# A two-layer attention trunk on one core: fixed tile places, memory keys in other banks, attention units in a new order, and one compressed-value product in place of four

## The chip, the cores and the metric

The kernel runs on one core of one Trainium2 chip. The metric is the device time of one execution in microseconds (us), as the median of several runs. A core has a matrix engine (PE, with its weight loads PEld), a vector engine (DVE), a scalar engine (ACT), a general engine (POOL) and a sync engine (SP), which here only issues DMAs. Each engine works through its own instructions in the order in which they were written down for it, and waits on semaphores for the others.

## What is computed

Two layers are applied to x (256 tokens, 1024 wide). In each, with h = RMSNorm(x) and z = h @ w_in:

```
o_a = nsa(q, kv, gate)       # 8 heads of 64, 2 key groups; three parts with a gate each:
                             #   compressed keys and values (15 blocks), selected blocks, a window
o_b = fox(q, k, v, f)        # 8 heads of 64, causal, with a forget bias
o_m = cross(q, mem_kv)       # 4 heads of 128 into 256 memory tokens
u   = sum over a, b, m of sigmoid(gate) * ((o * silu(.)) @ w_branch)
x   = x + u @ w_out
```

For the compressed part of `nsa` the kernel computes, for each of two groups of 128 tokens (t = 0, 1),

```
s   = einsum('bqgrd,bngd->bgrqn', qb, k_c) * scale       # n: 15 compressed blocks
p_c = masked_softmax(s, cmp_end <= t)
o_c = einsum('bgrqn,bngd->bqgrd', p_c, v_c)              # the product of the compressed values
```

where k_c and v_c come from k and v by a small two-layer network (`compress`). mem_kv = RMSNorm(mem) @ w_mem_kv gives the memory keys K and values V.

## The kernel before, in words

**Matrix products.** The large products run in `gemm_steps` (L264). An fp32 operand is split into a high and a low fp32r part, and three matmuls per 128 rows (high x high, low x high, high x low) accumulate in a bank of PSUM; `gemm` (L285) takes two banks, one for each t, from the pool `mm` (3 banks) unless another pool is given. PSUM has the pools mm (3 banks), S (2), T (2) and O (1) (L73). Weights come in granules of 256 rows and up to 512 columns: `load_w` (L123) has SP issue the DMA into one of four `wraw` tiles (L143), `split_w` (L147) has ACT write the high part `whi` (L172; L167 where a gain is multiplied in) and DVE the low part `wlo` (L173, L168). A granule is 12 matmuls.

**Order of the stages.** In a layer `mem_kv` (L466) comes first: K (L489), then V (L490). Then come the stages that `ORDER` (L30) names: K2 K1 Q (keys, values and queries of nsa), SA SB SM (silu gates, L848, 256-column matmuls), FK FQ FV (fox), MG (the first merge gate), MQ (memory queries); then branch a, b, m and w_out. A key bank of the memory is released when DVE has multiplied it with its norm (`kn`, L476), which waits for the norm `rmk` of POOL (L362 to L365).

**Units.** Attention is cut into units: scores on PE into an S bank, softmax on DVE and ACT, a last multiply of P by the inverse sum on POOL (L559), four transposes on PE (L228), a split into `PTh`/`PTl` (L382, L384), and products on PE into the O bank (L504). A queue of units is worked off in order, one is started per granule (`unit_step`, L241), and the head of the queue waits for the marks in its `deps`, with all units behind it. The queue before is: 4 units of t = 0, the compressed unit `Cmp` of t = 0, 8 units of t = 1, the `Cmp` of t = 1, the fox units, the memory units.

**The compressed unit** (L949) has 8 score matmuls (L962), a softmax, one transpose of `ce`, one 128x128 copy to `eT` (L349 on ACT or L351 on DVE, by turns) and four fp32 matmuls of 128 columns with the values `Vc` (L1003), one for each r, into one O bank. `Vc` is written in `value` (L922). The compress network runs during FK, through `compress_step` (L932) and a chain of small steps (L867 to L928).

**Tables.** While FK and the next stage run in layer 0, `smallp`, the small parameters of layer 1, is loaded (L607 to L609) once DVE has read the old ones for the last time (L908), and POOL builds 18 tables from it (L640 to L642).

**What sets the final order.** The program is written in Python in the order above; a scheduler then merges the instructions of all helpers into one order for each engine, by its own simulated times. So a change of the written order moves instructions on all engines. The pools give each tag its place in SBUF when it is first asked for.

Of the kernel before, what the change touches and what calls it, by code (L numbers as in the profile page):

```python
# [17 lines left out]
NT = 2  # L18
# [8 lines left out]
KEEP = 10  # L27
WARM = 8

ORDER = "K2 K1 Q SA SB FK MG FQ FV SM MQ".split()  # L30


def shape_constants():
    half = 32
    inv = (10000.0 ** (-np.arange(half, dtype=np.float32) / np.float32(half))).astype(np.float32)
    ang = np.arange(T, dtype=np.float32)[:, None] * inv[None, :]
    cos, sin = np.cos(ang).astype(np.float32), np.sin(ang).astype(np.float32)
    cos2 = np.concatenate([cos, cos], 1).reshape(NT, 128, 64).transpose(1, 0, 2)
    sin2 = np.concatenate([-sin, sin], 1).reshape(NT, 128, 64).transpose(1, 0, 2)
    ident = np.eye(128, dtype=np.float32)  # L40
    p = np.arange(128)
    ntri = -(p[:, None] <= p[None, :]).astype(np.float32)
    even = (p[:, None] == 2 * np.arange(64)[None, :]).astype(np.float32)
    odd = (p[:, None] == 2 * np.arange(64)[None, :] + 1).astype(np.float32)
    t = np.arange(T).reshape(NT, 128).T
    n = np.arange(15)
    cmask = np.where(16 * n[None, None, :] + 31 <= t[:, :, None], 0.0, NEG).astype(np.float32)

    bmask = 0.5 * (p[:, None] // 16 == np.arange(8)[None, :]).astype(np.float32)
    cm = np.where(p[None, :] <= p[:, None], 0.0, NEG).astype(np.float32)  # L50
# [10 lines left out]
def hybrid_kernel(ctx: ExitStack, tc, I, cst_d, out_d):  # L61
# [5 lines left out]
    def S(shape, tag, bufs=1, dt=F32):  # L67
        return sb.tile(shape, dt, tag=tag, name=tag, bufs=bufs)
# [3 lines left out]

    pmm, pS, pT, pO = bank("mm", 3), bank("S", 2), bank("T", 2), bank("O", 1)  # L73

    def T2():
        return S([128, 520], "t2", bufs=4)

    def SQ():
        return S([128, 512], "sq")
# [211 lines left out]
                between(g)  # L291


    cst = S([128, cst_d.shape[1]], "cst")
    mrow0 = S([128, NT, D], "big")

    def mem_cols(mrow, g):
# [23 lines left out]
    def take(n):  # L321
        off[0] += n
        return cst[:, off[0] - n:off[0]]
# [7 lines left out]
    bmask = take(8)  # L331
    cm = take(128)
    mhalf = S([128, 16], "mhalf")
    nc.gpsimd.memset(mhalf, -0.5)
# [131 lines left out]
    def mem_kv(l, mT, rm):  # L466
        KT = [S([128, 4, T], f"mK{i}", dt=F32R) for i in range(2)]
        V = [S([128, NT, 512], f"mV{i}", dt=F32R) for i in range(2)]

        def on_k(t, p):  # L470
            ss = ss_heads(p, 4, 128, scale=rm[t])
            r = rstd_of(ss, 128, "rmk", rm[t])

            def s1():
                kn = T2()[:, :512]
                nc.vector.tensor_tensor(heads(kn, 4), heads(p, 4), b3(r, 4, 128), op=ALU.mult)  # L476

                def s2():
                    ts = slice(t * 128, (t + 1) * 128)
                    put_T([lambda h=h: kn[:, h * 128:(h + 1) * 128] for h in range(4)],  # L480
                          lambda q: split_evac(KT[0][:, :, ts], KT[1][:, :, ts], q.rearrange("p (h t) -> p h t", h=4)))
                later(1 + t, s2)
            later(1, s1)

        def on_v(t, p):
            nc.scalar.activation(V[0][:, t], p, AF.Copy, scale=rm[t])
            nc.vector.scalar_tensor_tensor(V[1][:, t], p, rm[t], V[0][:, t].bitcast(F32), op0=ALU.mult, op1=ALU.subtract)

        gemm(mT, 8, on_k)  # L489
        gemm(mT, 8, on_v)  # L490
        return KT, V

# [100 lines left out]
    for l in range(2):  # L593
# [268 lines left out]
            mark((nm, l))  # L862


        Vc = S([128, 512], "Vc").rearrange("p (r g d) -> p r g d", r=4, g=2)

        def compress_out(i, hp):  # L867
            ch = S([128, 128], "cmph")
# [2 lines left out]
            def s1():  # L871
# [10 lines left out]
                def s2():  # L882
                    if i == 0:
                        sT = S([128, 30], "sT")
                        nc.vector.scalar_tensor_tensor(sT, th, 1.0, hs, op0=ALU.add, op1=ALU.mult)
                        later(1, lambda: key(sT))
                    else:
                        sT = S([128, 4, 2, 16], "sTv")
                        nc.gpsimd.memset(sT, 0.0)
                        nc.vector.scalar_tensor_tensor(hs, th, 1.0, hs, op0=ALU.add, op1=ALU.mult)  # L890
                        nc.vector.tensor_copy(sT[:, :, :, 0:15], heads(hs, 2)[:, None].to_broadcast([128, 4, 2, 15]))
                        later(1, lambda: value(sT))
                later(1, s2)

# [54 lines left out]
        class Cmp:  # L949
# [40 lines left out]

            def transpose(self):
                def out(q):
                    self.eT = S([128, 128], "eT")
                    evac(self.eT, q[:, 0:128])
                put_T([lambda: self.e.rearrange("p h n -> p (h n)")], out)

            def product(self):
                box = []

                def one(r):  # L1000
                    if not box:
                        box.append(pO())
                    nc.tensor.matmul(box[0][:, r * 128:(r + 1) * 128], Vc[:, r].rearrange("p g d -> p (g d)"), self.eT,  # L1003
                                     start=True, stop=True)
                for r in range(4):
                    put(lambda r=r: one(r), *([lambda: self.done(box[0])] if r == 3 else []))

        oa_ = act_pair(4, "oT")

        def nsa_units(t):  # L1010
# [7 lines left out]
                split_evac(oa_[0][:, :, ts], oa_[1][:, :, ts], s3)  # L1018
                mark(("oTa", l, t))

            deps = [("q", l, t)] + [("k", l, i, t_) for i in (1, 2) for t_ in range(t + 1)]
            res = []
            for g in range(2):
                gs = slice(g * 64, (g + 1) * 64)
                out = Out(2 if t == 0 else 4, lambda O, gs=gs: fold(sw, O, gs))
                for br in ((None,) if t == 0 else (0, 1)):
                    for r0 in (0, 2):
# [25 lines left out]
                        res.append(Unit(deps, score, *args, (0, 2, 1, 3), product))  # L1053
            res.append(Cmp(t, done_c))
            return res

# [161 lines left out]
        runs = dict(K1=run_k1, K2=run_k2, Q=run_q, MQ=run_mq,  # L1218
                    FK=lambda: gemm(hT, 8, on_fqk(fkT, False), between=compress_step),
                    FQ=lambda: gemm(hT, 8, on_fqk(fqT, True)),  # L1220
                    FV=lambda: (gemm(hT, 8, on_fv), mark(("fv", l))))
        for nm in ORDER:
# [55 lines left out]
```

## Time and profile before

| what | value |
|---|---|
| median of 3 runs | 636.09 us (635.55 to 636.16) |
| profiled execution, its own time | 636.09 us |
| its span in the trace | 634.4 us |
| PE busy | 621.8 us (98%) |
| DVE busy | 471.9 us (74%) |
| ACT busy | 382.0 us (60%) |
| POOL busy | 175.5 us (28%) |

PE is the engine of this kernel; the other engines prepare its operands. "Busy" of PE counts overlapping matmul records once, so the costs of PE work are read from the spacing of starts (a piece of the chain "start, length, what xN"), not from the mean of a record. Layer 0 takes the span up to about 306 us, and layer 1 repeats it. Engine letters, lines and shapes are as in the code; PEclk or the PEclk column is the granted clock of PE.

### The profile page before, as it was taken

What the parts mean: (1) busy time and instruction counts of PE and PEld (TensorE: products, weight loads), DVE (VectorE), ACT (ScalarE), POOL (GpSimd) and SP (SyncE); (2) the same over time, 40 slices, a digit from 0 to 9 for tenths busy, and PEclk for the clock granted to TensorE, in tenths of its full rate; (3) what the DMA queues carried; (4) which work ended last, traced back from release to release, by engine and by line L of the source; (5) the groups of instructions that cost most, each with busy time, mean ns of one, the idle gap of its engine ahead of it and who ended that gap; (6) DMA issues with size and microseconds to landing.
All of it is one profiled execution on the core that took longest, in us unless ns stands there. A gap on an engine that the chain in (4) does not pass through costs nothing.

```text
span 634.4 us, 10249 instructions
## 1 busy us (share of the span) xinstructions
PE 621.8 (98%) x3551; PEld 532.0 (84%) x3551; DVE 471.9 (74%) x844; ACT 382.0 (60%) x813; POOL 175.5 (28%) x234
## 2 busy tenths in 40 slices
PE   7899999999999999999999999999999999999997
PEld 5689998788998788888888989977889888888885
DVE  3668898668977886955577799966799678787563
ACT  5767567555666666555467656845566667664441
POOL 2813403242512320702112142141053051042130
PEclk8989999999999999999999999999999999999999
DMA  8788866275444545446855695445644465445541
GB/s 298 175 276 265 259 143 187 75 214 164 130 121 134 145 139 160 134 139 225 285 182 157 173 338 162 143 132 137 185 114 133 99 184 150 144 122 167 168 156 75
DMA packets 75189, 107.66 MB, mean 170 GB/s; under 512 B 16865, under 2 KB 30465, under 8 KB 74881
## 3 DMA queue, kind: packets, MB, share of 16 engines
q1 hardware_dynamic: 75072, 106.99, 56.7%
q8 instruction: 28, 0.46, 0.3%
q14 instruction: 25, 0.20, 0.1%
q10 hardware_dynamic: 64, 0.02, 0.0%
HBM read 103.82 MB, written 3.15 MB: 169 GB/s over the span
## 4 chain that ended last, share of the span: by engine, by line
PE 94%; DMA 3%; POOL 1%; SPq 0%; DVE 0%; issue 0%; ACT 0%; POOLq 0%
PE mm L274 60%; PE mm L848 11%; PE S L274 6%; PE T L228 6%; PE O L504 4%; PE S L1035 2%; DMA cst<-in_cst_dram 1%; PE S L1134 1%; PE S L942 1%; DMA big<-in_mem_dram 1%; PE S L1194 1%; DMA gcol<-in_fox_k_norm_dram 1%; PE S L1132 1%; PE O L1003 1%; PE S L962 1%; PE T L744 0%
## 5 line engine op out<-in xcount | busy, mean ns | idle before, releaser
L173 DVE TENSOR_TENSOR wlo<-wraw,whi 128x1024 fp32r<-128x1024 f32 (+2 forms) x160 | 200.8, 1258 | 79.9 <-ACT whi L172 78.6
L172 ACT ACTIVATE whi<-wraw 128x1024 fp32r<-128x1024 f32 (+2 forms) x160 | 166.8, 1042 | 101.7 <-PE mm L274 65.1
L274 PE MATMUL mm<-whi,aTh 128*128 128x512 f32 (+1 forms) x480 | 190.3, 399 | 2.1 <-DVE t L476 2.1
L274 PE MATMUL mm<-whi,aTl 128*128 128x512 f32 (+1 forms) x480 | 189.0, 394 | 0.3 <-DVE aTl L384 0.3
L274 PE MATMUL mm<-wlo,aTh 128*128 128x512 f32 (+1 forms) x480 | 184.6, 395 | 0.0
L559 POOL TENSOR_TENSOR P<-P,d 128x512 f32<-128x512 f32 (+1 forms) x64 | 61.1, 970 | 208.0 <-DVE d L555 104.6
L274 PEld LDWEIGHTS mm<-whi,aTh 128*128 128x128 f32 x480 | 90.5, 190 | 19.5 <-issue 3.2
L274 PEld LDWEIGHTS mm<-whi,aTl 128*128 128x128 f32 x480 | 90.8, 189 | 17.2 <-DVE aTl L384 0.7
L274 PEld LDWEIGHTS mm<-wlo,aTh 128*128 128x128 f32 x480 | 90.6, 189 | 16.8 <-issue 0.4
L848 PE MATMUL mm<-aTh,wlo 128*128 128x256 f32 x192 | 54.8, 287 | 0.0
L848 PE MATMUL mm<-aTl,whi 128*128 128x256 f32 x192 | 54.8, 286 | 0.0
L848 PE MATMUL mm<-aTh,whi 128*128 128x256 f32 x192 | 54.6, 285 | 0.0
L548 ACT ACTIVATE P<-S,m 128x256 f32<-128x256 f32 (+1 forms) x112 | 46.8, 428 | 7.4 <-DVE m L545 6.5
L1108 POOL TENSOR_TENSOR big<-big,t 128x512 f32<-128x512 f32 x16 | 27.9, 1752 | 59.2 <-DVE t L1107 54.2
L382 ACT ACTIVATE PTh<-T 128x512 fp32r<-128x512 f32 (+1 forms) x48 | 26.9, 561 | 25.6 <-PE T L228 25.4
L274 PE MATMUL mm<-whi,oTh 128*128 128x512 f32 x96 | 38.5, 404 | 0.7 <-ACT PTh L382 0.7
L274 PE MATMUL mm<-wlo,oTh 128*128 128x512 f32 x96 | 38.8, 407 | 0.0
L274 PE MATMUL mm<-whi,oTl 128*128 128x512 f32 x96 | 38.6, 402 | 0.0
L848 PEld LDWEIGHTS mm<-aTh,wlo 128*128 128x128 f32 x192 | 36.5, 191 | 0.4
L848 PEld LDWEIGHTS mm<-aTh,whi 128*128 128x128 f32 x192 | 36.6, 190 | 0.3
L848 PEld LDWEIGHTS mm<-aTl,whi 128*128 128x128 f32 x192 | 36.6, 190 | 0.2
L545 DVE TENSOR_REDUCE m<-S 128x2 f32<-128x512 f32 (+3 forms) x64 | 32.3, 515 | 2.7 <-PE S L1194 2.5
(232 smaller groups left out, 1033.0 us busy)
## 6 DMA issues: line engine op xcount, KB each, us to landing
wraw<-in_w_in_dram SPq DMA_DIRECT2D x112, 512.0 KB, 3.8
wraw<-in_w_out_dram SPq DMA_DIRECT2D x16, 512.0 KB, 4.3
wraw<-in_w_mem_kv_dram SPq DMA_DIRECT2D x15, 512.0 KB, 5.2
wraw<-in_w_branch_a_dram SPq DMA_DIRECT2D x16, 256.0 KB, 3.9
wraw<-in_w_branch_b_dram SPq DMA_DIRECT2D x8, 512.0 KB, 3.6
wraw<-in_w_branch_m_dram SPq DMA_DIRECT2D x8, 512.0 KB, 3.6
wraw<-in_w_in_dram SPq DMA_DIRECT2D x8, 408.0 KB, 4.2
wraw<-in_w_in_dram SPq DMA_DIRECT2D x8, 384.0 KB, 3.8
```

The costliest lines, as they stand in the source:

```text
L172: nc.scalar.activation(wh[:, j, :n], v[:, j, :n], AF.Copy)
L173: nc.vector.tensor_tensor(wl[:, j, :n], v[:, j, :n], wh[:, j, :n].bitcast(F32), op=ALU.subtract)
L228: nc.tensor.transpose(q[0][0:b.shape[1], i * 128:(i + 1) * 128], b, ident)
L274: mi = nc.tensor.matmul(o_, a[:, kg, ts], w_[:, k, :n], start=(kg == 0 and i == 0), stop=(last and k == 1 and i == 2))
L382: nc.scalar.activation(hi, src, AF.Copy, scale=scale)
L504: nc.tensor.matmul(self.O[0:lhsT.shape[1], cols], lhsT, rhs, start=first, stop=False, skip_group_check=True)
L545: nc.vector.tensor_reduce(m[:, n:n + c], heads(sp[:, o_:o_ + w * c], c), axis=AXX, op=ALU.max, negate=True)
L548: nc.scalar.activation(self.P[:, k], sp[:, k], AF.Exp, bias=m[:, n:n + 1], accum_out=d[:, n:n + 1])
L559: nc.gpsimd.tensor_tensor(P3, P3, b3(d[:, n:n + c], c, w), op=ALU.mult)
L848: mi = nc.tensor.matmul(o_, w_, a[:, kg, :], start=(kg == 0 and j % 2 == 0 and i == 0), stop=(kg == 7 and i == 2), skip_group_check=True)
L1035: put(lambda j=j, k_=k_: nc.tensor.matmul(sp()[:, j * 256:(j + 1) * 256], QA[:, g, r0 + j, ts], k_, start=(j == 0 and k_ is kh), stop=(j = ...
L1108: nc.gpsimd.tensor_tensor(uv, uv, tn, op=ALU.add)
```

## The change

The change has five parts.

1. Thirty tags get their places first, in one list with fixed sizes; `t2` has 512 columns and not 520, the constants' tile is 832 wide, and the mask `bmask` has 2 columns and not 8.
2. In layer 0 the memory keys accumulate in the two S banks (`bank=None if l else pS`), and V takes the mm banks.
3. The queue of units begins with the 4 units of t = 0, then the 8 of t = 1, and only then the two `Cmp` units. The 8 units wait for the end of FK by a new mark.
4. `ORDER` has MG after FQ and FV.
5. The compressed values' product is one fp32r matmul of 96 rows and 512 columns. Rows 0 to 31 hold the high part of the values against the high part of P, rows 32 to 63 high against low, rows 64 to 95 low against high. Twelve pieces of 32x128 (8 on ACT, 4 on DVE) write `eT`, now in a `PTh` tile, where one copy did.

```
-ORDER = "K2 K1 Q SA SB FK MG FQ FV SM MQ".split()
+ORDER = "K2 K1 Q SA SB FK FQ FV MG SM MQ".split()
...
-    bmask = 0.5 * (p[:, None] // 16 == np.arange(8)[None, :]).astype(np.float32)
+    bmask = 0.5 * ((p[:, None] // 16) % 2 == np.arange(2)[None, :]).astype(np.float32)
...
+    for tag, width, bufs, dt in (("cst", 832, 1, F32), ("big", 2048, 1, F32), ("wraw", 1024, 4, F32), ("whi", 1024, 3, F32R),
...
+        S([128, width], tag, bufs, dt)
...
-        gemm(mT, 8, on_k)
+        gemm(mT, 8, on_k, bank=None if l else pS)
         gemm(mT, 8, on_v)
...
-        Vc = S([128, 512], "Vc").rearrange("p (r g d) -> p r g d", r=4, g=2)
+        V3 = S([128, 128], "V3", dt=F32R)[0:96]
...
-                nc.tensor.matmul(vp[:, 0:64], sT.rearrange("p r g n -> p (r g n)"), w2[:, 1, :], start=True, stop=True)
-                nc.vector.tensor_tensor(Vc.rearrange("p r g d -> p (r g) d"), vp[:, 0:64][:, None, :].to_broadcast([128, 8, 64]), b3(bmask, 8, 64),
-                                        op=ALU.mult)
+                nc.tensor.matmul(vp[0:96, 0:64], sT.rearrange("p r g n -> p (r g n)"), w2[:, 1, :], start=True, stop=True)
+                vf = S([128, 128], "cmph")[0:96]
+                nc.vector.tensor_tensor(heads(vf, 2), vp[0:96, 0:64][:, None, :].to_broadcast([96, 2, 64]), b3(bmask[0:96], 2, 64),
+                                        op=ALU.mult)
+                nc.scalar.activation(V3, vf, AF.Copy)
+                nc.vector.tensor_tensor(V3[64:96], vf[64:96], V3[64:96].bitcast(F32), op=ALU.subtract)
...
-                    self.eT = S([128, 128], "eT")
-                    evac(self.eT, q[:, 0:128])
+                    self.eT = eT = S([128, 512], "PTh", bufs=2, dt=F32R)[0:96]
+                    for r in range(4):
+                        rs, src = slice(r * 128, (r + 1) * 128), q[r * 32:(r + 1) * 32, 0:128]
+                        nc.scalar.activation(eT[0:32, rs], src, AF.Copy)
+                        nc.vector.tensor_tensor(eT[32:64, rs], src, eT[0:32, rs].bitcast(F32), op=ALU.subtract)
+                        nc.scalar.activation(eT[64:96, rs], src, AF.Copy)
...
-                    nc.tensor.matmul(box[0][:, r * 128:(r + 1) * 128], Vc[:, r].rearrange("p g d -> p (g d)"), self.eT,
-                                     start=True, stop=True)
-                for r in range(4):
-                    put(lambda r=r: one(r), *([lambda: self.done(box[0])] if r == 3 else []))
+                    nc.tensor.matmul(O, V3, self.eT, start=True, stop=True)
+                    self.done(O)
+                put(one)
...
-        for t in range(NT):
-            units.extend(nsa_units(t))
+        nu_ = [nsa_units(t) for t in range(NT)]
+        for u_ in nu_[1][:-1]:
+            u_.deps.append(("FK", l))
+        units.extend(nu_[0][:-1] + nu_[1][:-1] + [nu_[0][-1], nu_[1][-1]])
...
+                    FK=lambda: (gemm(hT, 8, on_fqk(fkT, False), between=compress_step), mark(("FK", l))),
```

Lines from the list of tags on are 11 higher in the changed kernel (L274 becomes L285), those behind `value` some 15.

On POOL in layer 0, before: behind the norm `cr` of the compressed keys the tables of layer 1 stand in one run, and the multiplies of P of the units of t = 1 come behind them (names: Ct and St are the tables, P a unit's probabilities, rf a norm of FQ).

```order
L903 TENSOR_TENSOR cr<-cr,mhalf 30x1
L640 TENSOR_TENSOR Ct<-cst,smallp 128x64
L641 TENSOR_TENSOR St<-cst,smallp 128x32
...
L642 TENSOR_TENSOR St<-cst,smallp 128x32
L889 MEMSET sTv 128x128
L559 TENSOR_TENSOR P<-P,d 128x512 x2
```

The same place with the change: one multiply, 6 tables, one multiply, 12 tables, the four steps of FQ's norms, and the third multiply.

```order
L570 TENSOR_TENSOR P<-P,d 128x512
L651 TENSOR_TENSOR Ct<-cst,smallp 128x64
...
L653 TENSOR_TENSOR St<-cst,smallp 128x32
L570 TENSOR_TENSOR P<-P,d 128x512
L651 TENSOR_TENSOR Ct<-cst,smallp 128x64
...
L653 TENSOR_TENSOR St<-cst,smallp 128x32
L373 TENSOR_SCALAR rf<-ss 128x8
L374 TENSOR_TENSOR rf<-rf,mhalf 128x8
L373 TENSOR_SCALAR rf<-ss 128x8
L374 TENSOR_TENSOR rf<-rf,mhalf 128x8
L570 TENSOR_TENSOR P<-P,d 128x512
```

So the second and third units of t = 1 now have tables ahead of their multiply.

On PE at the start of layer 0, before, with the numbers of the tiles: mm_145 and mm_146 hold K for t = 0 and 1, mm_315 and mm_316 V. mm_316 takes the bank that mm_145 held, so that its first matmul waits for K of t = 0 to be read (L476).

```order
L274 MATMUL mm_315<-whi_319,aTh_107 128x512
L274 MATMUL mm_315<-whi_319,aTl_108 128x512
L274 MATMUL mm_316<-whi_226,aTh_107 128x512
L274 MATMUL mm_316<-whi_226,aTl_108 128x512
L274 MATMUL mm_316<-wlo_227,aTh_107 128x512
L274 MATMUL mm_316<-whi_226,aTh_107 128x512
L274 MATMUL mm_316<-whi_226,aTl_108 128x512
L274 MATMUL mm_316<-wlo_227,aTh_107 128x512
L228 MATMUL T_372<-cst_63,t2_311 128x128 x4
```

The same place with the change: both halves of V go on together, granule by granule, and the transposes of the normed keys (T_402) come 30 V matmuls behind the last of K's.

```order
L285 MATMUL mm_346<-whi_349,aTh_137 128x512
L285 MATMUL mm_346<-whi_349,aTl_138 128x512
L285 MATMUL mm_345<-wlo_350,aTh_137 128x512
L285 MATMUL mm_345<-whi_349,aTh_137 128x512
L285 MATMUL mm_345<-whi_349,aTl_138 128x512
L285 MATMUL mm_346<-wlo_350,aTh_137 128x512
L285 MATMUL mm_346<-whi_349,aTh_137 128x512
L285 MATMUL mm_346<-whi_349,aTl_138 128x512
L239 MATMUL T_402<-cst_93,t2_341 128x128 x4
```

The V matmuls of three granules now stand ahead of those transposes, in banks that K does not use.

On ACT in layer 0, with the change, the pieces of the first `Cmp` unit (L1012 and L1014, PTh 32x128) stand among other work; before there was one copy here.

```order
L1012 ACTIVATE PTh<-T 32x128
L994 ACTIVATE ce<-csm 128x8x15
L1014 ACTIVATE PTh<-T 32x128
L1012 ACTIVATE PTh<-T 32x128
L183 ACTIVATE whi<-wraw 128x1024
L559 ACTIVATE P,d<-S,m 128x128
L1014 ACTIVATE PTh<-T 32x128
L1012 ACTIVATE PTh<-T 32x128
L587 ACTIVATE tm<-O 64x512
L1108 ACTIVATE t_1930<-mm 128x512
L559 ACTIVATE P,d<-S,m 128x256
L1014 ACTIVATE PTh<-T 32x128
```

Behind these rows follow one more L1012, one L183, one L1108 and the last L1014 of the unit. On PE the unit's transpose stands 57 matmuls ahead of its product: 17 of L285 with 512 columns, 31 of L859 with 256 columns, 4 of L515, 4 of L1148 and L1150, and the transpose of the second `Cmp`.

## Rows read from the trace of the kernel before

**Rows 1.** The page: busy time by engine, and the chain's shares by engine.

```profile
PE 621.8 (98%) x3551; PEld 532.0 (84%) x3551; DVE 471.9 (74%) x844; ACT 382.0 (60%) x813; POOL 175.5 (28%) x234
...
PE 94%; DMA 3%; POOL 1%; SPq 0%; DVE 0%; issue 0%; ACT 0%; POOLq 0%
```

**Rows 2.** What PE waited for: us in total, times, longest us.

```profile
PE mm L274 <- DVE t L476: 2.1, 1, 2.1
...
PE mm L274 <- ACT PTh L382: 0.7, 2, 0.3
```

**Rows 3.** The chain in order of time: start us, length us, what.

```profile
59.22 10.92 PE mm L274 x48
...
92.86 4.91 PE mm L848 x41
...
159.16 0.89 PE O L1003 x8
```

**Rows 4.** Line L1003 on PE: duration ns min/median/max, first and last start us.

```profile
L1003 PE MATMUL O<-eT,Vc x32: 271/275/275, 159.0 to 500.1; 128*128 128x128 f32 x32
```

**Rows 5.** Timeline of the start: start us, length us, instruction [idle before <-releaser].

```profile
30.15 0.69 DVE L476 TENSOR_TENSOR t<-mm,rmk 128x512 f32<-128x512 f32 x1 [2.88 <-POOL rmk L365]
...
30.99 0.47 PE L274 MATMUL mm<-whi,aTh 128*128 128x512 f32 x1 [2.06 <-DVE t L476]
...
33.46 1.33 ACT L167 ACTIVATE whi<-wraw,gk 128x512 fp32r<-128x512 f32 x2 [1.06 <-DMA wraw<-in_w_mem_kv_dram]
...
34.01 0.63 PE L274 MATMUL mm<-whi,aTl 128*128 128x512 f32 x1
...
34.22 1.42 DVE L168 SCALAR_TENSOR_TENSOR wlo<-wraw,gk,whi 128x512 fp32r<-128x512 f32 x2 [0.70 <-ACT whi L167]
...
37.25 0.90 ACT L172 ACTIVATE whi<-wraw 128x832 fp32r<-128x832 f32 x1 [1.98 <-DMA wraw<-in_w_in_dram]
...
38.19 1.03 DVE L173 TENSOR_TENSOR wlo<-wraw,whi 128x832 fp32r<-128x832 f32 x1 [1.96 <-ACT whi L172]
...
41.51 0.35 PE L274 MATMUL mm<-wlo,aTh 128*128 128x416 f32 x1
```

**Rows 6.** Work by stretch: PE, PEld, DVE, ACT, POOL busy, PEclk, DMA share, GB/s.

```profile
31.00:70.00 39.00, 39.00 (x193) 35.09 (x194) 30.95 (x80) 24.35 (x59) 8.32 (x13) 0.96 0.88 279
```

**Rows 7.** Small reads of PSUM, lines L685 and L687: columns as in rows 4.

```profile
L685 ACT ACTIVATE KH<-T x16: 254/273/276, 57.9 to 389.6; 64x128 fp32r<-64x128 f32 x16
...
L687 DVE TENSOR_TENSOR KL<-T,KH x16: 269/285/295, 59.2 to 392.1; 64x128 fp32r<-64x128 f32 x16
```

**Rows 8.** ACT groups by form: busy us, mean ns, idle before.

```profile
L172 ACT ACTIVATE whi<-wraw 128x1024 fp32r<-128x1024 f32 x144 | 152.8, 1061 | 95.7 <-PE mm L274 62.3 <-issue 10.8 <-PE mm L848 7.5
L548 ACT ACTIVATE P<-S,m 128x256 f32<-128x256 f32 x64 | 29.7, 471 | 7.2 <-DVE m L545 6.5 <-DVE d L555 0.7
L548 ACT ACTIVATION_READ_ACCUMULATOR P<-S,m 128x1 f32 x112 | 23.0, 205 | 0.0
...
L1092 ACT ACTIVATE t<-mm 128x512 f32<-128x512 f32 x24 | 14.2, 592 | 9.3 <-PE mm L274 9.1
```

**Rows 9.** Timeline of layer 0 around the tables, of PE, SP, POOL and DVE.

```profile
124.97 0.30 PE L897 MATMUL T<-w,sT 128*30 128x64 f32 x2
...
128.24 0.34 SPq L607 DMA_DIRECT2D smallp<-in_nsa_q_norm_dram  x1
...
131.65 0.32 POOL L640 TENSOR_TENSOR Ct<-cst,smallp 128x64 f32<-128x64 f32 x1 [3.94 <-DMA smallp<-in_nsa_q_norm_dram]
131.93 0.25 POOL L641 TENSOR_TENSOR St<-cst,smallp 128x32 f32<-128x32 f32 x1
...
134.90 1.40 DVE L173 TENSOR_TENSOR wlo<-wraw,whi 128x1024 fp32r<-128x1024 f32 x1 [1.95 <-ACT whi L172]
...
135.17 1.31 POOL L640 TENSOR_TENSOR Ct<-cst,smallp 128x64 f32<-128x64 f32 x1
...
157.23 1.65 POOL L363 TENSOR_TENSOR rf<-rf,mhalf 128x8 f32<-128x8 f32 x1
```

More of the change, by code (lines that the diff above doesn't have):

```diff
@@ L73, in hybrid_kernel @@
     pmm, pS, pT, pO = bank("mm", 3), bank("S", 2), bank("T", 2), bank("O", 1)
+    for tag, width, bufs, dt in (("cst", 832, 1, F32), ("big", 2048, 1, F32), ("wraw", 1024, 4, F32), ("whi", 1024, 3, F32R),
+                                 ("wlo", 1024, 3, F32R), ("aTh", 2048, 2, F32R), ("aTl", 2048, 2, F32R),
+                                 ("oTh", 1024, 2, F32R), ("oTl", 1024, 2, F32R), ("P", 512, 2, F32R), ("PTh", 512, 2, F32R),
+                                 ("PTl", 512, 2, F32R), ("KH", 1024, 1, F32R), ("KL", 1024, 1, F32R), ("VN", 1024, 1, F32R),
+                                 ("mK0", 1024, 1, F32R), ("mK1", 1024, 1, F32R), ("mV0", 1024, 1, F32R),
+                                 ("mV1", 1024, 1, F32R), ("fV", 2048, 1, F32R), ("t2", 512, 4, F32), ("t4", 1024, 2, F32),
+                                 ("x0", 1024, 1, F32), ("x1", 1024, 1, F32), ("tm", 512, 2, F32), ("Lc", 1024, 1, F32),
+                                 ("sg", 1024, 2, F32), ("o", 512, 2, F32), ("sq", 512, 1, F32), ("Vc", 512, 1, F32)):
+        S([128, width], tag, bufs, dt)
     def T2():
-        return S([128, 520], "t2", bufs=4)
+        return S([128, 512], "t2", bufs=4)
     def SQ():
@@ L291, in gemm @@
                 between(g)
-    cst = S([128, cst_d.shape[1]], "cst")
+    cst = S([128, 832], "cst")[:, :cst_d.shape[1]]
     mrow0 = S([128, NT, D], "big")
@@ L330, in hybrid_kernel @@
     cmask = take(30).rearrange("p (t n) -> p t n", t=2)
-    bmask = take(8)
+    bmask = take(2)
     cm = take(128)
@@ L887, in s2 @@
                     else:
-                        sT = S([128, 4, 2, 16], "sTv")
+                        sT = S([128, 3, 2, 16], "sTv")
                         nc.gpsimd.memset(sT, 0.0)
                         nc.vector.scalar_tensor_tensor(hs, th, 1.0, hs, op0=ALU.add, op1=ALU.mult)
-                        nc.vector.tensor_copy(sT[:, :, :, 0:15], heads(hs, 2)[:, None].to_broadcast([128, 4, 2, 15]))
+                        nc.vector.tensor_copy(sT[:, :, :, 0:15], heads(hs, 2)[:, None].to_broadcast([128, 3, 2, 15]))
                         later(1, lambda: value(sT))
@@ L992, in out, with one @@
                 def out(q):
-                    self.eT = S([128, 128], "eT")
-                    evac(self.eT, q[:, 0:128])
+                    self.eT = eT = S([128, 512], "PTh", bufs=2, dt=F32R)[0:96]
[4 more added lines that the diff above has]
+                        nc.scalar.activation(eT[64:96, rs], src, AF.Copy)
                 put_T([lambda: self.e.rearrange("p h n -> p (h n)")], out)
             def product(self):
[L998 to L1002, printed above, removed]
-                    nc.tensor.matmul(box[0][:, r * 128:(r + 1) * 128], Vc[:, r].rearrange("p g d -> p (g d)"), self.eT,
-                                     start=True, stop=True)
-                for r in range(4):
-                    put(lambda r=r: one(r), *([lambda: self.done(box[0])] if r == 3 else []))
+                def one():
+                    O = pO()
+                    nc.tensor.matmul(O, V3, self.eT, start=True, stop=True)
+                    self.done(O)
+                put(one)
         oa_ = act_pair(4, "oT")
@@ L1019, in done_c @@
                 mark(("oTa", l, t))
-            deps = [("q", l, t)] + [("k", l, i, t_) for i in (1, 2) for t_ in range(t + 1)]
+            deps = lambda: [("q", l, t)] + [("k", l, i, t_) for i in (1, 2) for t_ in range(t + 1)]
             res = []
@@ L1052, in nsa_units @@
                                     lambda h0=h0, br=br: gat[:, t, h0:h0 + 2, 1 + br])
-                        res.append(Unit(deps, score, *args, (0, 2, 1, 3), product))
+                        res.append(Unit(deps(), score, *args, (0, 2, 1, 3), product))
             res.append(Cmp(t, done_c))
@@ L1218, in hybrid_kernel @@
         runs = dict(K1=run_k1, K2=run_k2, Q=run_q, MQ=run_mq,
-                    FK=lambda: gemm(hT, 8, on_fqk(fkT, False), between=compress_step),
+                    FK=lambda: (gemm(hT, 8, on_fqk(fkT, False), between=compress_step), mark(("FK", l))),
                     FQ=lambda: gemm(hT, 8, on_fqk(fqT, True)),
```

## The prediction

> **What bounds the kernel now.** I read the page first: PE is busy 98% of the span and the chain of work that ended last runs over PE for 94% [rows 1]. So an edit pays if it takes work from PE, or if it ends a wait of PE; work of other engines counts only where it makes PE wait. The list of PE's waits, read second, is short [rows 2]: in the middle of the program stand 2.1 us for the memory keys' norm at the start, once, and 0.7 us for a unit's `PTh`. The chain in order of time, read third, gives prices: a 512-column fp32r matmul takes 10.92 / 48 = 0.227 us of PE, a 256-column one 4.91 / 41 = 0.120, and one whole compressed product, four fp32 matmuls of 128 columns in 8 records, 0.89 [rows 3]. The timeline of the start, read last, shows what lies around the one long wait [rows 5].
>
> The sum is made against the profiled execution: 636.09 us, of which 634.4 is the span and 1.7 lies around it. It is also the median of the runs.
>
> **The product.** There are 32 records of L1003 [rows 4], 8 for each product, so four products in all (two groups of tokens, two layers). Each costs 0.89 us, and the new matmul has 512 columns of fp32r. A row with 96 rows of depth doesn't exist in the trace; the nearest, 512 columns with 128 rows, is 0.227 [rows 3], and I take that. If depth 96 were no better than the old way the gain would be nothing, but column count alone tells the spacing of the rows with 256 and 512 columns. Four times 0.89 - 0.227 gives **-2.65 us**. All of it lies on PE, hence on the path.
>
> What the product needs is dearer now: 12 pieces in place of one copy. The nearest rows, 64x128 from PSUM, take 0.273 us on ACT and 0.285 on DVE [rows 7], so 8 x 0.273 + 4 x 0.285 = 3.3 us per product. Is it covered? On PE 57 matmuls stand between the transpose and the first product of a layer: 17 x 0.227 + 31 x 0.120 = 7.6 us, and 9 others of some 0.12 to 0.3, about 1.6; 9.2 in all. On ACT, from the unit's first piece to its last, stand 8 pieces (2.2), two `whi` splits at 1.06, two exponentials with their reads and the one for `ce`, at most 3 x 0.47 + 2 x 0.2, and three PSUM reads of 512 columns at 0.59 [rows 8]: 7.9 us. It fits by 1.3 us, so I cost it at nothing; the cover is thin, and is the second rival. The three new instructions that make `V3` stand in the compress chain, tens of us ahead of the product.
>
> **The start.** Before, V's second half needs the bank of K's first half. DVE frees it at L476, which waits 2.88 us for `rmk`, and PE idles 2.06 us until 30.99 [rows 5]. With K in the S banks, V runs on. What is late next? The last memory weights: ACT splits them from 33.46, DVE until 34.22 + 1.42 = 35.64. So V's last 12 matmuls can't start before 33.46 + 0.67 = 34.1 and end near 34.1 + 12 x 0.227 = 36.9; then come 8 transposes, about 0.9 us, and K2. K2's first weights are ready as high part at 37.25 + 0.90 = 38.15, as low part at 38.19 + 1.03 = 39.22. Both rest on a DMA, not on V. K2's first matmul with the low part began at 41.51; now it may begin at 39.22. The ceiling is 2.3 us. I take **-2.2**, since later weights have two or more us in hand. The lower bound: PE now idles twice for about a microsecond, before V's last weights and before K2. Before, a 512-column matmul at 34.01 shows 0.63 us, and the stretch 31 to 70 has a clock of 0.96 [rows 5, 6]: after the idle the clock stood at its lower level, 1.2 in place of 2.4 GHz, for (1 - 0.96) x 39 / 0.5 = 3 us, which costs 1.5 us. Then it hid behind late weights; if it now falls in K2, 0.7 of the gain is left. Bounds: -0.7 to -2.3.
>
> **The order of stages and units.** Instructions are the same, only their places change. The eight units of t = 1 start at the end of FK, not behind the first `Cmp`, so they are done earlier and fewer waits are left for branch a. The 0.7 us of waits for `PTh` [rows 2] may go: I take **-0.7**. As bounds I take twice that as a gain (waits too short for the list), -1.4, and +1.5 as a loss: some five new waits as long as the longest of that kind, 0.3 us.
>
> **At nothing.** Fixed places issue no instruction. `smallp` is loaded two granules earlier on SP, ahead of weights that are wanted only several granules later. A constants' table with 6 columns less changes no wait.
>
> **The sum.** 636.09 - 2.65 - 2.2 - 0.7 = **630.5 us**.
>
> **The tables on POOL.** The second and third unit of t = 1 now wait behind 6 and 12 tables and four norm steps. Tables wait for `smallp`. Before, it was 3.3 us from L897 to the issue of that load and 3.4 more to the first table (124.97, 128.24, 131.65) [rows 9]. By the changed order of PE, with the spacings above, the second unit's scores end as L897 runs; its transposes come 19.6 us later, the third's 24.6 us later. From 7 us on POOL has 18 tables at some 0.27, two norms at 1.65 and small steps, two multiplies at about 1: some 11 us. So the second unit's multiply is done at 10 and the third's at 18, and 6.5 us are left. A table that met a `wlo` split, however, took 1.31 us in place of 0.32: it began at 135.17 in the split that ran from 134.90 to 136.30, and ended with it [rows 9]. Each such meeting costs 1.0 us, so seven of them are needed for a loss. A split can hold up one table only, and some five splits fall in that stretch: no loss in the sum.
>
> The Trainium skill, SBUF — State Buffer, section "SBUF: two separate sides", says that DVE instructions with two inputs in SBUF and GpSimd instructions share a port pair that one of them holds for its whole instruction. By that rule, the 1.31 us is a wait for a lock, as the trace shows, and the change brings more units' work of DVE beside the tables; were all 18 held, the sum would be the third rival's.
>
> **The rivals.**
>
> 1. *The clock falls in K2.* For it: two idles of about a microsecond where one of 2.06 was followed by slow matmuls. Against it: they are shorter. The start then gives 0.7: 636.09 - 2.65 - 0.7 - 0.7 = 632.0. Chance 0.14.
> 2. *The pieces are late: slower.* The first product of a layer has 1.3 us in hand on ACT. But the exponentials among the pieces wait for DVE's maxima; such waits sum to 6.5 us [rows 8], and two of 1.6 us each would make 7.9 + 3.2 = 11.1 against 9.2: 1.9 us late. DVE's four pieces, too, are queued behind `wlo` splits. PE has only in-order work behind the product, so it stands. It decides from 1.7 us per product on; if all four are 1.9 late, 630.5 + 7.6 = 638.1. Against it: the scheduler spread PE's order with pieces in mind, and the second product's cover is longer. Chance 0.05. Half of it would give 634.3.
> 3. *The tables are held up: slower.* All 18 tables meet a split: 18 x 1.0 - 6.5 = 12 us, 642. Against it: there aren't that many splits in the stretch. Chance 0.02.
> 4. *The new order makes stalls that eat the gain.* DVE is busy 74% on average [rows 1] and strictly in order; with eight units' softmax moved together into FQ and FV, splits of weights may come late by 4 to 5 us in all: about 635.5, no difference. Chance 0.08.
>
> **How the numbers follow.** The forecast has 0.71, with its own range of 628.9 (636.09 - 2.65 - 2.3 - 1.4, less a little) to 633. With the first rival it covers 0.85 of the cases: the range of 628.4 to 633.8 also takes in half-late pieces at one layer. A measurement of this kernel can tell about 0.2%, 1.3 us, from no change. Faster is the forecast and the first rival, 0.85; same the fourth, 0.08; slower the second and third, 0.07.
>
> **What would show it.** Right: the product stands as one record with a spacing near 0.23 us, four times; PE's wait for L476 is gone, K2 starts near 38.2 and Q's 48 matmuls, before at 59.22 [rows 3], near 57.0; no new wait of PE above 0.5 us names `PTh` from the pieces or a P. Wrong: a wait of PE ahead of the product by a piece, a P multiply of POOL in layer 0 that ends after its place on PE, or a granted clock under 1 in K2.

## The result, and the profile after

The changed kernel takes 630.73 us (median of 4 runs, 630.26 to 631.0) against 636.12 of the kernel before in the same runs: ratio 0.9921, 95% interval 0.9909 to 0.9933. The profiled execution took 631.0 us with a span of 629.1. The forecast was 630.5 with a range of 628.4 to 633.8. The total came out as forecast. Of its three terms that of the product held, that of the start was there at first and gone by 75 us, and the third, the order's, was right in its cause and not in its size, as the experiments show.

The page of the kernel after: busy time by engine, and the chain's shares by engine, which answer to [rows 1].

```profile
PE 617.2 (98%) x3523; PEld 527.4 (84%) x3523; DVE 475.6 (76%) x860; ACT 389.6 (62%) x845; POOL 168.3 (27%) x234
...
PE 90%; DMA 4%; POOL 3%; issue 1%; DVE 1%; SPq 0%; ACT 0%; POOLq 0%; ACTq 0%; DVEq 0%
```

PE has 28 records less (32 products' records against 4), DVE 16 and ACT 32 more: the pieces and what makes `V3`, less the old copies. POOL is now 3% of the chain, and that is new.

The list of what PE waited for, after (us in total, times, longest us), answers to [rows 2].

```profile
PE T L239 <- DMA big<-in_mem_dram: 2.3, 1, 2.3
PE mm L285 <- ACT whi L178: 1.7, 2, 1.1
PE S L329 <- DVE P L326: 1.5, 1, 1.5
PE mm L285 <- DVE t L1088: 0.8, 1, 0.8
PE T L239 <- DVE t L665: 0.7, 1, 0.7
PE mm L285 <- DVE wlo L184: 0.4, 1, 0.4
PE mm L859 <- DVE t L428: 0.3, 1, 0.3
PE T L239 <- DVE ncs L803: 0.2, 1, 0.2
```

The two waits that the prediction named, for the memory keys' norm (2.1 us) and for `PTh` at branch a (0.7), are gone. Three others matter below: L1088 is DVE's multiply with FQ's norm; L428 and `ncs` stand in the stage of the silu gates, at 74 us.

The new product, in the timeline of the kernel after (start us, length us, instruction): the last piece, the product, and the next instruction on PE.

```profile
182.90 0.27 ACT L1014 ACTIVATE PTh<-T 32x128 fp32r<-32x128 f32 x1
...
185.30 0.40 PE L1020 MATMUL O<-PTh,V 96*128 96x512 f32 x1
185.54 0.49 PE L239 MATMUL T<-cst,P 128*128 128x128 f32 x3
```

The next start comes 0.24 us behind the product's, where four fp32 matmuls took 0.89 [rows 3]. The last piece ended at 183.17, and the product was due at 185.30: 2.1 us in hand. The other three products have 2.1 to 2.2 us in hand as well.

### The profile page after: what moved, and what is told of

Read it like the earlier page. It is cut to its first block, busy times and chain, and to the rows that moved or that the text cites. A ratio compares the mean times of both kernels' runs of the same rounds, so it can differ in the third digit from the quotient of the medians.

```text
span 629.1 us, 10230 instructions
## 1 busy us (share of the span) xinstructions
PE 617.2 (98%) x3523; PEld 527.4 (84%) x3523; DVE 475.6 (76%) x860; ACT 389.6 (62%) x845; POOL 168.3 (27%) x234
## 4 chain that ended last, share of the span: by engine, by line
PE 90%; DMA 4%; POOL 3%; issue 1%; DVE 1%; SPq 0%; ACT 0%; POOLq 0%; ACTq 0%; DVEq 0%
PE mm L285 57%; PE mm L859 11%; PE S L285 6%; PE T L239 5%; PE O L515 4%; PE S L1051 2%; DMA smallp<-in_nsa_k_norm_dram 1%; DMA wraw<-in_w_in_dram 1%; PE S L1150 1%; DMA big<-in_mem_dram 1%; PE S L957 1%; PE S L1210 1%; POOL Ct L651 1%; PE S L1148 1%; DMA gcol<-in_mem_q_norm_dram 1%
## 5 line engine op out<-in xcount | busy, mean ns | idle before, releaser
L184 DVE TENSOR_TENSOR wlo<-wraw,whi 128x1024 fp32r<-128x1024 f32 (+2 forms) x160 | 198.0, 1241 | 75.5 <-ACT whi L183 73.5
L183 ACT ACTIVATE whi<-wraw 128x1024 fp32r<-128x1024 f32 (+2 forms) x160 | 166.6, 1042 | 95.4 <-PE mm L285 62.3
L285 PE MATMUL mm<-whi,aTh 128*128 128x512 f32 (+1 forms) x464 | 182.7, 396 | 2.6 <-ACT whi L178 1.7
L285 PE MATMUL mm<-whi,aTl 128*128 128x512 f32 (+1 forms) x464 | 182.8, 394 | 0.0
L285 PE MATMUL mm<-wlo,aTh 128*128 128x512 f32 (+1 forms) x464 | 176.7, 393 | 0.5 <-DVE wlo L184 0.4
L285 PEld LDWEIGHTS mm<-whi,aTh 128*128 128x128 f32 x464 | 87.1, 188 | 20.1 <-ACT whi L178 2.4
L570 POOL TENSOR_TENSOR P<-P,d 128x512 f32<-128x512 f32 (+1 forms) x64 | 57.8, 914 | 170.6 <-DVE d L562 80.2
L285 PEld LDWEIGHTS mm<-wlo,aTh 128*128 128x128 f32 x464 | 87.1, 188 | 16.8 <-DVE wlo L184 1.5
L285 PEld LDWEIGHTS mm<-whi,aTl 128*128 128x128 f32 x464 | 87.3, 188 | 15.9 <-DVE aTl L397 0.4
L859 PE MATMUL mm<-aTh,wlo 128*128 128x256 f32 x192 | 55.6, 291 | 0.0
L859 PE MATMUL mm<-aTh,whi 128*128 128x256 f32 x192 | 54.7, 285 | 0.3 <-DVE t L428 0.3
L859 PE MATMUL mm<-aTl,whi 128*128 128x256 f32 x192 | 54.6, 285 | 0.0
L559 ACT ACTIVATE P<-S,m 128x128 f32<-128x128 f32 (+1 forms) x112 | 47.0, 429 | 11.8 <-DVE m L556 10.4
L285 PE MATMUL mm<-whi,oTh 128*128 128x512 f32 x96 | 38.4, 400 | 0.0
L285 PE MATMUL mm<-whi,oTl 128*128 128x512 f32 x96 | 37.8, 394 | 0.0
L859 PEld LDWEIGHTS mm<-aTh,whi 128*128 128x128 f32 x192 | 36.7, 191 | 1.0 <-DVE t L428 0.5
L285 PE MATMUL mm<-wlo,oTh 128*128 128x512 f32 x96 | 37.0, 392 | 0.0
L859 PEld LDWEIGHTS mm<-aTh,wlo 128*128 128x128 f32 x192 | 36.6, 191 | 0.3
L859 PEld LDWEIGHTS mm<-aTl,whi 128*128 128x128 f32 x192 | 36.7, 191 | 0.2
L395 DVE TENSOR_TENSOR PTl<-T,PTh 128x512 fp32r<-128x512 f32 (+1 forms) x48 | 30.8, 641 | 5.7 <-ACT PTh L393 5.5
```

Of the source, the lines that this page charges most:

```text
L183: nc.scalar.activation(wh[:, j, :n], v[:, j, :n], AF.Copy)
L184: nc.vector.tensor_tensor(wl[:, j, :n], v[:, j, :n], wh[:, j, :n].bitcast(F32), op=ALU.subtract)
L285: mi = nc.tensor.matmul(o_, a[:, kg, ts], w_[:, k, :n], start=(kg == 0 and i == 0), stop=(last and k == 1 and i == 2))
L395: nc.vector.tensor_tensor(lo, src, hi.bitcast(F32), op=ALU.subtract)
L559: nc.scalar.activation(self.P[:, k], sp[:, k], AF.Exp, bias=m[:, n:n + 1], accum_out=d[:, n:n + 1])
L570: nc.gpsimd.tensor_tensor(P3, P3, b3(d[:, n:n + c], c, w), op=ALU.mult)
```

## The experiments

Every ratio is to the kernel before, timed beside it; its 95% interval stands in brackets. "Worth" means the difference of two ratios times 636 us. First each part was taken out of the changed kernel, then each was put alone into the kernel before.

**Without the bank.** The memory keys go back to `mm`.

```
-        gemm(mT, 8, on_k, bank=None if l else pS)
+        gemm(mT, 8, on_k)
```

> The changed kernel, but the memory keys of layer 0 go back to the mm banks; all else stays. The prediction's sum (the bank is worth 2.2 us): 632.9 us. Theory read from the two traces (the early start of K2 is given back to new waits for weights and to transposes that now come behind it, so the bank is worth about 1.0): 631.7 us. Rival (the start is bound by weights in any case, the bank is worth nothing): 630.7 us.

Measured: 633.5 us, 0.9976 [0.9962, 0.9991], with 12 executions spread from 631.67 to 636.85. By the medians the bank is worth 3.5 us, more than the wait that it removes (2.1) and more than any of the three forecasts. A later experiment shows where they lie: not at the start.

**Without the product.** `Vc`, the four fp32 matmuls and the single copy `eT` are put back in the changed kernel.

```
-                    nc.tensor.matmul(O, V3, self.eT, start=True, stop=True)
-                    self.done(O)
+                    nc.tensor.matmul(box[0][:, r * 128:(r + 1) * 128], Vc[:, r].rearrange("p g d -> p (g d)"), self.eT,
+                                     start=True, stop=True)
```

> The changed kernel with the old compressed product (four fp32 matmuls, one copy to eT, Vc). The prediction's sum (2.65 us for four products): 633.4 us. Theory from the traces (the product and the fewer switches between fp32 and fp32r matmuls are worth 3.2 us): 633.9 us. Rival (the twelve pieces cost as much elsewhere as the product gives): 631.5 us or less.

Measured: 633.31 us, 0.9967 [0.9955, 0.998]. The product is worth 2.9 us; 4 x (0.89 - 0.24) = 2.6 by the spacings. The intervals are too wide to part the prediction's 2.65 from the theory's 3.2.

**Without the new queue and order.** `ORDER` and the queue of units as before.

```
-ORDER = "K2 K1 Q SA SB FK FQ FV MG SM MQ".split()
+ORDER = "K2 K1 Q SA SB FK MG FQ FV SM MQ".split()
...
-        units.extend(nu_[0][:-1] + nu_[1][:-1] + [nu_[0][-1], nu_[1][-1]])
+        for t in range(NT):
+            units.extend(nsa_units(t))
```

> The changed kernel with the old queue of units and the old order of stages (MG before FQ). The prediction's sum (the order is worth 0.7 us): 631.4 us. Theory from the traces (branch a loses its waits, some 3 us over two layers, but FK and the place behind the tables lose nearly as much): 630.7 us, within 0.6. Rival (the order carries the gain): 633 us or more.

Measured: 645.08 us, 1.0147 [1.0132, 1.0161]: slower than the kernel before by 9.3 us. Priced at 0.7, the part is worth 14.4 once the product is there; of the three forecasts only the rival's bound, 633 us or more, holds that.

**Without the places.** No list of tags, `t2` with 520 columns; every engine's instructions stand in the same order.

```
-    for tag, width, bufs, dt in (("cst", 832, 1, F32), ("big", 2048, 1, F32), ("wraw", 1024, 4, F32), ("whi", 1024, 3, F32R),
...
-        S([128, width], tag, bufs, dt)
```

> The changed kernel without the list of tags and with the old sizes of t2 and the constants' tile. Its instructions and their order on every engine are those of the changed kernel; only addresses differ. Both the prediction and the theory from the traces: 630.7 us, within 0.5. Rival (addresses decide what collides): more than 1.3 us off.

Measured: 631.87 us, 0.9945 [0.9933, 0.9957]; worth 1.5 us, where the prediction had nothing. The two intervals touch, so this rests on the spacing of matmuls further down as well.

**Each part alone in the kernel before.** `b_bank` has the one line with `pS`, `b_prod` only the product, `b_units` only the queue and `ORDER`; places as before in all three. Their edits are the three diffs above, read the other way.

> The kernel before with the memory keys of layer 0 in the S banks, nothing else. The prediction's sum: 636.1 - 2.2 = 633.9 us. Theory from the traces (1.0): 635.1 us. Rival (the start is bound by weights): 636.1 us.

> The kernel before with the new compressed product alone (its queue of units has the first Cmp between the units of t = 0 and t = 1). The prediction's sum: 633.4 us. Theory from the traces (3.2): 632.9 us. Rival (with the old queue the twelve pieces are late for the product, 1.7 us or more each): 636 us or more.

> The kernel before with the new queue of units and the new order of stages, nothing else. The prediction's sum (0.7): 635.4 us. Theory from the traces (gain in branch a and loss in FK and FQ nearly cancel): 636.1 us, within 0.6. Rival (the order carries the gain): 634 us or less.

Measured: 636.3 us, 1.0016 [1.0007, 1.0024]; 648.2 us, 1.0199 [1.0186, 1.0212]; 637.83 us, 1.0039 [1.0023, 1.0055]. Each part alone is slower than the kernel before, by 1.0, 12.7 and 2.5 us, and together with the places they are 5.0 us faster. The bank and the queue came out slower than any of their three forecasts (the queue with a wide spread, 635.88 to 640.35 us); for the product the rival was right. So the terms are not a sum. The next experiments show that the product needs the queue, and that the bank gives nothing once the tables are away.

**The queue or the stage order?** One kernel takes only the old `ORDER` into the changed kernel, the other only the old queue.

```
-ORDER = "K2 K1 Q SA SB FK FQ FV MG SM MQ".split()
+ORDER = "K2 K1 Q SA SB FK MG FQ FV SM MQ".split()
```

> The changed kernel with the old order of stages (MG before FQ and FV), the new queue of units kept. Theory (FQ and FV early feed the fox units before the pieces of the compressed units crowd ACT; the stage order carries what undoing both cost): 640 us or more. Rival (the queue, with both compressed units behind the 8 units of t = 1, carries it): 633 us or less.

```
-        units.extend(nu_[0][:-1] + nu_[1][:-1] + [nu_[0][-1], nu_[1][-1]])
+        for t in range(NT):
+            units.extend(nsa_units(t))
```

> The changed kernel with the old queue of units (a compressed unit behind the units of each t, no wait for the end of FK), the new order of stages kept. Theory (the stage order carries it): 633 us or less. Rival (the queue carries it): 640 us or more.

Measured: 631.84 us, 0.994 [0.9927, 0.9954], and 645.38 us, 1.0152 [1.0138, 1.0166]. The theory that the stage order carries the product fell: the queue is worth 14.7 us, `ORDER` 1.2 (and the intervals of that one overlap). The kernel with the old queue shows a reason, in its timeline around the second compressed unit (columns as above, in brackets the idle time before and its releaser).

```profile
195.88 0.27 PE L239 MATMUL T<-cst,ce 128*128 128x128 f32 x1
...
196.25 0.27 ACT L1012 ACTIVATE PTh<-T 32x128 fp32r<-32x128 f32 x1 [0.49 <-PE T L239]
...
199.65 0.56 DVE L395 TENSOR_TENSOR PTl<-T,PTh 128x384 fp32r<-128x384 f32 x1
...
199.93 0.27 ACT L1012 ACTIVATE PTh<-T 32x128 fp32r<-32x128 f32 x1
...
200.35 0.45 PE L239 MATMUL T<-cst,P 128*128 128x128 f32 x1 [2.07 <-DVE PTl L395]
```

The compressed unit's transpose lands in one of the two T banks at 195.88. Its 12 pieces are still being read at 199.93: the bank is held for over 4 us, and the units' transposes have one T bank left. With the old queue the transposes of other units come right then, one after the other into that bank, and PE stands 2.07 us until DVE has read it. In the kernel after, the pieces of the first compressed unit hold their bank even longer, from 175.69 to 183.17, but PE has only one other transpose in that time, that of the second compressed unit.

```profile
175.69 0.27 PE L239 MATMUL T<-cst,ce 128*128 128x128 f32 x1
...
181.67 0.27 PE L239 MATMUL T<-cst,ce 128*128 128x128 f32 x1
```

The work by stretch (start:end, length, then PE, PEld, DVE, ACT, POOL busy, PEclk, DMA share, GB/s) of the kernel with the old queue:

```profile
170.00:215.00 45.00, 42.86 (x287) 39.15 (x286) 40.45 (x90) 32.65 (x86) 12.69 (x20) 0.92 0.31 82
```

and of the kernel after:

```profile
170.00:215.00 45.00, 45.00 (x285) 40.24 (x285) 40.64 (x92) 34.63 (x97) 11.65 (x20) 1.00 0.48 129
```

PE idles 2.14 us, and the granted clock is 0.92 on average: with the wait it falls to 0.50, 1.2 GHz in place of 2.4, for 6.8 us (here the kernel with the old queue),

```profile
199.60:206.40 6.80, 6.05 (x24) 5.15 (x25) 5.52 (x16) 4.00 (x14) 1.94 (x4) 0.50 0.00 0
```

which costs half of them, 3.4 us. Layer 1 repeats it (470 to 530: clock 0.94 against 1.00, PE idle 2.22, so 2.2 + 3.4). Both layers give 11.2 us of the 13.6 by which the spans of the two traces differ (642.7 and 629.1). Of the rest, 0.6 us are a longer wait for L1088 (1.48 against 0.84) and 0.7 a new one for L1174; the remainder is not traced. With the product alone in the kernel before, the same stretch has a clock of 0.92 too; there PE waits elsewhere, for exponentials of the fox units on ACT,

```profile
PE S L1137 <- ACT P L548: 5.5, 2, 2.8
```

and in the timeline pieces of the second compressed unit stand on ACT ahead of these exponentials: seven of them since 193.79, 2.0 us in all.

```profile
197.73 0.27 ACT L1001 ACTIVATE PTh<-T 32x128 fp32r<-32x128 f32 x1
...
198.39 0.47 ACT L548 ACTIVATE P<-S,m 128x256 f32<-128x256 f32 x1
...
199.00 0.80 PE L1137 MATMUL S<-aTl,aTh 65*128 65x128 f32 x2 [2.77 <-ACT P L548]
```

The kernel with both the old queue and the old `ORDER` has the same wait (3.5 us in two). So by these traces the pieces of the second unit are what PE stands for with the old queue, at a T bank with the new `ORDER` and at ACT with the old one. That the queue decides is measured; this path is read from the traces, and no run varied it alone.

**The tables later.** Two small POOL additions that read the tables' tiles and a late value of u hold the 18 tables back until branch a; PE, DVE, ACT and SP keep their order.

```
+        if l == 0:
+            hold = S([128, 2], "hold")
+            for i, t_ in enumerate((Ct, St)):
+                nc.gpsimd.tensor_tensor(hold[:, i:i + 1], t_[:, 0, 0, 0:1], u[:, 1, 1023:1024], op=ALU.add)
```

> The changed kernel, with the 18 tables of layer 1 held back on POOL until branch a of layer 0 (two 128x1 adds that read the old tables and a late result stand ahead of them); the order on PE, DVE, ACT and SP is that of the changed kernel. Theory from the traces (the wait of PE for DVE's L1088, 1.0 us with what follows, comes from FQ's norm behind 12 tables on POOL): 629.7 us and that wait gone. Rival (FQ's norm is late for another reason, the sums of squares or DVE's order): 630.7 us and the wait still there.

Measured: 629.66 us, 0.9909 [0.9897, 0.9922], worth 0.8 us by the medians (the intervals overlap). The chain of the kernel after (start us, length us, what) shows what it removes.

```profile
125.92 3.50 issue
129.45 1.02 POOL Ct L651
...
133.31 1.27 POOL Ct L651
...
136.49 0.21 POOL rf L373
...
136.78 1.65 POOL rf L374
...
138.45 0.70 DVE t L1088
...
139.19 3.01 PE mm L285 x12
```

POOL stood 3.5 us for `smallp`, then the tables came, and FQ's norm `rf` had 18 of them ahead of it. DVE's L1088 waited 2.40 us for `rf`, and PE 0.84 for L1088. With late tables the norm is done 2 us earlier, on POOL and DVE of that kernel:

```profile
134.79 1.64 POOL L374 TENSOR_TENSOR rf<-rf,mhalf 128x8 f32<-128x8 f32 x1
...
136.46 0.69 DVE L1088 TENSOR_TENSOR t<-mm,rf 128x512 f32<-128x512 f32 x1 [0.15 <-POOL rf L374]
```

and its list of PE's waits names L1088 no more, as the theory had it.

**The tables later, and no bank.** The edit above (the two POOL additions), with `gemm(mT, 8, on_k)` as well: the memory keys go back to `mm`.

> The changed kernel with the memory keys back in the mm banks, and the 18 tables of layer 1 held back on POOL as before (two 128x1 adds ahead of them). Theory (without the new bank the changed kernel lost its 3 us not at the start but in FQ, where tables on POOL made PE wait and its clock fall): 630.5 us, within 0.8, and no wait of PE at the end of FQ. Rival (the 3 us are the start's): 632.5 us or more.

Measured: 628.28 us, 0.9888 [0.9875, 0.9902]: faster than the theory's 630.5, within 0.8, and by the medians 1.3 us faster than with the bank and late tables (0.9909; the intervals overlap). So once the tables are away the bank gives nothing, and its 3.5 us are not at the start. Holding the tables back is worth 5.6 us without the bank (0.9976 to 0.9888) and 0.8 with it. The chain from 56 us on, first of the kernel without the bank (tables not held back):

```profile
58.85 10.92 PE mm L285 x48
69.77 3.11 PE mm L859 x26
...
73.64 0.26 PE T L239
73.90 1.19 PE mm L859 x10
75.08 0.11 PE T L239
75.19 2.87 PE mm L859 x24
```

and of the kernel after:

```profile
57.68 1.85 PE mm L285 x8
...
69.21 4.07 PE mm L859 x34
...
73.82 0.23 PE T L802 x2
...
74.08 0.41 DVE ncs L803
74.49 0.33 DVE t L427
74.82 0.34 DVE t L428
...
75.20 2.90 PE mm L859 x22
```

Both have 36 of L859's matmuls behind them at about 75 us (26 + 10, and 2 + 34). With the bank PE reached Q at 57.68, 1.2 us ahead of 58.85; the 37th of L859 starts at 75.20 with the bank and, in the timeline, at 74.95 without it (a piece of the chain begins where the one before it ends, hence 75.19). So the lead is gone. PE ran through the 36 without a break, ten more of them ahead of the forget gates' transposes (L800 to L802) than without the bank, and then nothing was left to fill the time in which DVE copies `ncs` and makes the two reads behind it (L427, L428), for which a bank of `mm` waits. `ncs` began at 74.08, and in the kernel before at 74.05. It waits for PE's L802, and PE came to these transposes at 73.21 without a wait, behind the ten more matmuls. In their old place they would have had to wait: what they transpose comes from a chain of small steps on DVE, whose last (`lf`, L794) ended at 72.90, before at 71.28, so 1.6 us later though PE was ahead. DVE was busy 18.39 of the 20 us from 57 to 77 (before 17.27), and had the chain's steps later in its order. No run varied that order alone; that the lead is gone is measured, that the new orders of DVE and PE take it is read from the trace.

Where most of the 3.5 us lie shows the stretch 125 to 160 of three kernels (columns as above): without the bank,

```profile
125.00:160.00 35.00, 32.77 (x165) 26.98 (x164) 28.97 (x53) 21.14 (x48) 16.89 (x30) 0.90 0.46 126
```

after,

```profile
125.00:160.00 35.00, 34.16 (x186) 28.70 (x185) 30.12 (x53) 24.52 (x51) 15.86 (x29) 1.00 0.51 153
```

and with late tables and no bank.

```profile
125.00:160.00 35.00, 35.00 (x193) 29.76 (x192) 31.81 (x59) 24.84 (x51) 12.82 (x13) 1.00 0.54 156
```

Without the bank the scheduler sets POOL's order otherwise, the tables meet FQ's norms worse, PE idles 2.2 us and the clock falls to 0.90 on average, (1 - 0.90) x 35 = 3.5 us more. With the tables away neither remains. This trace is of an execution of 635.36 us with a granted clock of 0.991 over the whole; seven of the 12 executions of that kernel have 0.997 and a median of 633.16. So the fall of the clock came in some executions only, and without it the bank is still worth some 2.7 us.

**The places again.** The tiles `aTh` and `aTl` are placed last, at the upper end of a partition.

```
-                                 ("wlo", 1024, 3, F32R), ("aTh", 2048, 2, F32R), ("aTl", 2048, 2, F32R),
+                                 ("wlo", 1024, 3, F32R),
...
+                                 ("aTh", 2048, 2, F32R), ("aTl", 2048, 2, F32R)):
```

> The changed kernel with aTh and aTl last in the list of tags, so that these stationary operands lie at 183680 to 216448 bytes and not at 68992 to 101760; the instructions and their order on every engine are the same. Theory (a stationary operand that lies in the upper part of a partition makes a 512-column matmul some 5 ns longer, as oTh and oTl show, 233 against 227 to 228 ns; some 1500 matmuls read aT): 637 us, within 2. Rival (the places of oT matter for another reason, its neighbours or what runs then): 630.7 us, within 0.7.

Measured: 630.39 us, 0.9924 [0.9911, 0.9936], as the kernel after, and as the rival had it. The groups by form (busy us, mean ns, idle before) show one of the groups of the three branch products, without the places:

```profile
L274 PE MATMUL mm<-wlo,oTh 128*128 128x512 f32 x96 | 37.5, 397 | 0.0
```

and the same in the kernel after; with `aTh` high it has 392 too.

```profile
L285 PE MATMUL mm<-wlo,oTh 128*128 128x512 f32 x96 | 37.0, 392 | 0.0
```

The spacing of starts is the better measure: 233.3 ns on average for the 288 matmuls with `oTh` or `oTl` in the kernel before and without places, 228.0 to 228.5 in those with places (neighbours less than 0.26 us apart). 288 x 5.3 ns is 1.5 us, the measured worth. The ones with `aTh` or `aTl` take 228.5 at either place, so the height of that operand in the partition isn't the cause. What fits all kernels, by the places that the pools give, is the distance from `oTh` to `whi`: a multiple of 1024 bytes where the spacing is short, 51008 and 51520 bytes where it is long. No run varied that distance alone; it stays open.

## Why the prediction was right, and where it was not

**The product, -2.65: right.** 2.6 by the spacing of 0.24 us (0.227 was taken), 2.9 by the run without it.

**The cover of the pieces: right in size, thin in reason.** On ACT 7.2 us passed from the first piece to the last, 7.9 were priced; 2.1 us were in hand, against 1.3. But the step counted only what hides the pieces on ACT. What else waits was left out: the T bank that the pieces hold, and the exponentials behind them on ACT. That the cover exists is due to the queue of part 3: without it the second product of each layer has 0.2 to 0.9 us in hand, and the kernels with the new product are 9 to 13 us slower than the kernel before. The second rival had the sign of that, at a smaller price (638.1). It sought the place on ACT; that is where PE's wait ends in the two kernels with the old `ORDER`, ahead of a fox unit's scores and not of the product, while with the new `ORDER` it ends at a T bank.

**The start, -2.2: wrong in the end.** What was forecast for the start itself came: L476's wait went, PE idled 1.07 and 0.41 us in its place, K2 began at 38.61 (38.2 forecast), Q at 57.68 (57.0), the clock from 31 to 70 us was 1.00, so the first rival's fall in K2 did not come. The step that failed is "later weights have two or more us in hand". It looked at weights alone. Next were DVE's own reads of banks, behind the forget-gate chain: at 75 us nothing of the lead is left. Alone in the kernel before, the bank costs 1.0 us, and with late tables the kernel without it is the faster.

**The order, -0.7: mechanism right, size off.** The waits for `PTh` at branch a went, worth 0.57 us a layer in the spacing of starts there, 1.15 in all. Against it stands the new wait of 0.84 us for FQ's norm, about 1.0 with what follows. As a part on which the others rest, the queue is worth 14.7 us, which a price by its own waits could not show.

**The tables: no loss forecast, 0.8 to 1.0 us lost.** The step took the units' multiplies of P as the ones that wait; no wait of PE in the kernel after names one. It counted the norms' time on POOL but not who waits for them: `rf` stands behind the tables too, and DVE's L1088 and a bank of `mm` wait for `rf`. As for the tables' own time, two of 18 took 1.02 and 1.31 us in place of some 0.3, each beside a `wlo` split of DVE. The Trainium skill, SBUF — State Buffer, section "SBUF: two separate sides", says that a DVE instruction with two inputs in SBUF and a GpSimd instruction that reads SBUF exclude each other, as one of them holds the shared port pair for its whole length; those two rows agree with it. A delay of all 18, the third rival, did not come.

**The places, nothing: wrong by 1.5 us** in the spacing of 288 matmuls, as above.

So the sum held by luck: the start's 2.2 us went and 1.0 was lost at FQ's norm, and gains that the prediction had at nothing (the places, the end of the span) or too small (branch a) made up for them. The spans differ by 5.3 us (634.4 to 629.1). In starts of the same matmul of the large products the changed kernel is 1.5 us ahead when layer 1 has begun (at 299 us) and 4.55 at the end. Layer 0 has product 1.3, places 0.75, branch a 0.57 and 0.1 at 75 us (75.20 against 75.33 before for the 37th matmul of L859), less 1.0 for FQ's norm: 1.7 us where the starts show 1.5. Layer 1 has the first three, 2.6 us where they show 3.1; these two differences are not traced. The last 0.7 us lie at the end, where from PE's last start to the end of the span pass 4.28 us, before 5.0; no experiment touched that.

## What to carry to other kernels

An early start is a gain only as far as the next engine in order allows: after the weights, look at what DVE must read for PE to get its banks back, and carry the lead forward to the next place where PE stands. Count for each new small read how long it holds its PSUM bank, and who else uses that pool, not only the reading engine's time. And parts of such a change are not to be priced one by one: here each alone is slower than the kernel before, together they are faster, and without one of them (the bank), with the tables late, the kernel has the lowest median of all that were measured, 628.28 us.

## What was not expected of the hardware

The same 512-column fp32r matmuls, in the same order, took 233.3 or 228.0 to 228.5 ns from start to start, depending only on where their tiles lie in SBUF. And idle time of PE of 2.1 to 2.2 us in a stretch of 35 to 45 us came with a granted clock of 0.90 to 0.92, which cost more (3.4 to 3.5 us) than the idle time itself; with one kernel (the one without the bank) in some of its executions only. From 31 to 70 us, with no wait for the norm, the clock was 1.00, before 0.96 [rows 6].
